# A 3x3 convolution with max-pooling: 23 of 32 steps with four products, sums from PSUM, and a new order

## The chip, the cores and the metric

The kernel runs on one core of one Trainium2 chip. The metric is the device time of one execution in microseconds (us), the median of several runs; less is better.

## The reference

16 images of 64 channels and 64x64 pixels are convolved with 128 filters of 3x3 (zero padding of one), and each 2x2 block of the result is reduced to its maximum, all in fp32:

```
x_pad = np.pad(x, ((0, 0), (0, 0), (1, 1), (1, 1)))
conv[b, co] += weight[co, ci, kh, kw] * x_pad[b, ci, kh:kh+h, kw:kw+w]     # over ci, kh, kw
output[b, c, i, j] = max of conv[b, c, 2*i:2*i+2, 2*j:2*j+2]               # 16 x 128 x 32 x 32
```

## The kernel before

**Steps.** Two images lie side by side in the 128 partitions (2 x 64 channels). A pair of images is cut into four quarters of 16 rows (eight pairs of rows, R = 8), which makes 8 x 4 = 32 steps. TensorE works on the two images (halves h = 0 and 1) at the same time, each with 64 rows of its array; a result of 128 filters x 8 rows x 64 columns fills one of eight PSUM banks (`acc`).

**Products.** A step needs the convolution's even rows and odd rows. Three taps (kw = 0, 1, 2) with one set of weights and one operand make a *product*: three matmuls for each half, six in all. Written plainly a step would have six products (two output rows by three kh); the kernel shares work between the two rows in two ways:
- a **K step** has five products. PA1 and PA2 make one difference of the outputs and PB1 and PB2 the other, straight from bf16 rows (`kx`), with weights D2, G0, D0, G2. PR adds the common part from `ks`, the sum of an even and an odd row (KS, VectorE, line 301), after the maximum of the two has been taken.
- a **W step** has four: P2 (weights GM, operand `we`, the difference of even and odd rows), P0 and P3 (weights G0 and G2, operand `wd`, differences of rows two apart) and P1 (weights GP, operand `ws`, the sum of even and odd rows). The operands are made from fp32 rows (`wx`): E makes `we` (on VectorE for the steps in `DIFF_ON_VECTOR`, else POOL, line 332), D makes `wd` (POOL, line 341), WS makes `ws` (VectorE; line 315 as a reduction over pairs for the steps in `SUM_BY_REDUCTION`, else line 323 as a sum of two SBUF operands).

**After the products.** For each half of a step: SE (W steps, line 411) is a copy of P2's bank into a second bank by ScalarE, to which P0 or P3 add. EV (lines 399 and 401) copies one bank to SBUF (`ev`) by ScalarE, with the sign changed in W steps. MX (line 427, VectorE) takes the maximum of the other bank and `ev`, in place. PR or P1 adds the common part. OD (line 431, ScalarE) copies the odd columns to SBUF, CM (line 437, VectorE) takes the maximum with the even columns into `o`, and `o` is stored.

**Order.** Nothing is scheduled by the compiler: `ORDER` is one list of step names, and each engine executes its own instructions in the order of the list. `PA1.2.1` is PA1 of step 2, half 1. A product is held until the other half has one too; then their matmuls alternate. The DMA queue of SP takes loads (`L`) and stores in the list's order as well; `LK` loads K rows as bf16 through POOL's queue; `LB` is a load held behind the last VectorE operation with two SBUF operands. POOL's operations are also held behind the last such VectorE operation (`on_vector` and `on_gpsimd`).

**The head.** Step 0 is a K step, the first W step (step 1 before) follows it. To start early both are done in halves of four rows:
- SP loads the weights (`wraw`), the first quarter in two parts (`kfirst`) and then, in the order of `first_loads = (1, 2,)`, the second K quarter (`ksecond`) and the first W step's rows in two parts (`wx`), whichever step comes first in number.
- The weights are combined (D2, D0, GM, GP on VectorE; g0, g1, g2 on ScalarE; GS on POOL; uG1, uGM, uGP on POOL), turned on TensorE (TD2, TG0, ...) and brought back to SBUF as bf16 (VD2, VG0, VGM, ...).
- XOa, XOb, XEa, XEb cast the first quarter's odd and even rows; X1 and X2 cast `ksecond` on ScalarE.
- F.k.part are the four products of step 0 (k = 0: D2, 1: G0, 2: D0, 3: G2), part 0 and 1; G.k.part those of the first W step (k = 0: P2, 1: P0, 2: P3).
- Ea and Eb (VectorE, line 353) and Da and Db (POOL, line 368) make that W step's operands by halves; SEa and SEb seed by halves.

These lines set the order of the first loads and the rule by which POOL waits:

```
first_loads = (1, 2,)
for s in first_loads:
    if s == KSTEPS[1]:
        nc.sync.dma_start(out=ksecond, in_=rows_of(0, klo2, khi2))
    else:
        wload(s, 0)
        wload(s, 1)
```

Of the kernel before, what the change touches and what calls it, by code (L numbers as in the profile page):

```python
# [11 lines left out]
def kernel(  # L12
# [103 lines left out]
    ksecond = const.tile([128, khi2 - klo2, W], FP32)  # L116
    first_loads = (1, 2,)
# [52 lines left out]
    def turn_out(m):  # L170
        free.append(turned[m])
        lo, hi, src = turned_cols(m)
        dst = wt[:, lo:hi, :].rearrange("p a b -> p (a b)")
        if m == "GM":
            nc.scalar.mul(dst, src, 0.5)
        elif m == "GP":
            nc.vector.tensor_scalar_mul(out=dst, in0=src, scalar1=0.5)
        elif m in ("G0", "G2"):
            nc.scalar.copy(out=dst, in_=src)
        else:  # L180
            nc.vector.tensor_copy(out=dst, in_=src)  # L181

# [85 lines left out]
    def first_product(k, part):  # L268
        s, q = KSTEPS[0], 0
        m0, first, where, skip = (  # L270
            (D2, 1, ta, None),
            (G0, -1, ta, 0),
            (D0, 0, tb, None),
            (G2, 2, tb, None),
        )[k]
        span = (0, R // 2) if part == 0 else (R // 2, R)
        start = k in (0, 2) and part == 0
        if start:
            take(where, s, 0)
            take(where, s, 1)  # L280
        pair_of_taps(where, s, m0, step2(kx_of(s), first), start, skip, span)
# [27 lines left out]

    def ws(s):  # L310
        row["ws", s] = ws_pool.tile([128, R, W], BF16, name="ws")
        t, f = wx_rows(s)
        if s in SUM_BY_REDUCTION:
# [14 lines left out]
    def we(s):  # L328
        row["we", s] = e_pool.tile([128, R, W], BF16, name="we")
        t, f = wx_rows(s)  # L330
        vector = s in DIFF_ON_VECTOR
        inst = (nc.vector if vector else nc.gpsimd).tensor_tensor(  # L332
# [43 lines left out]
    def lk(n, part):  # L376
# [3 lines left out]
        if n == 0:  # L380
            inst = kload(0, *chunk(2 + part))
            if part == 0:
                behind(inst, sbuf_op[0])
        elif part == 0:
# [8 lines left out]
    ev, od, ot, made = {}, {}, {}, {}  # L393
# [39 lines left out]
    def colmax(s, h):  # L433
# [5 lines left out]
        made[s] = made.get(s, 0) + 1  # L439
# [3 lines left out]
        if s == N - 1:  # L443
            store = nc.scalar if made[s] == 1 else nc.sync
            store.dma_start(out=dst[:, h : h + 1], in_=src[:, h : h + 1])
        elif made[s] == 2:
            nc.sync.dma_start(out=dst, in_=src)


    def cast_rows(lo, hi):  # L450
        on_vector(nc.vector.tensor_copy(out=kx[0][:, lo:hi:2, :], in_=kfirst[:, lo:hi:2, :]))  # L451

    def cast_more(first):
# [7 lines left out]
        "g0": lambda: nc.scalar.copy(out=slots(G0), in_=g0),  # L461
        "g1": lambda: nc.scalar.copy(out=slots(G1), in_=g1),  # L462
        "g2": lambda: nc.scalar.copy(out=slots(G2), in_=g2),
# [3 lines left out]
        "GM": lambda: on_vector(nc.vector.tensor_sub(out=slots(GM), in0=gsum, in1=g1)),  # L467
        "GP": lambda: on_vector(nc.vector.tensor_add(out=slots(GP), in0=gsum, in1=g1)),
        "XOa": lambda: cast_rows(1, kmid),
        "XOb": lambda: cast_rows(kmid, khi),  # L470
        "XEa": lambda: cast_rows(0, kmid),
        "XEb": lambda: cast_rows(kmid + 1, khi),
# [11 lines left out]
        "SE": seed, "EV": evac, "MX": rowmax, "OD": odd, "CM": colmax,  # L484
    }
# [4 lines left out]
    for m in PRODUCTS:  # L490
# [3 lines left out]
        D0 g2 g1 TD0 TG2 g0 D2 XEa LB.3 LB.4 PR.0.1 TD2 VG2 PA1.2.1 VD0 TG0 uG1 TG1 GS F.2.0 VD2 XOa LB.6  # L494
        LB.8 LB.9 GM VG0 F.3.0 XOb F.0.0 uGM F.1.0 VG1 F.0.1 TGM PA2.2.1 XEb LK.0.0 F.1.1 F.2.1 F.3.1 VGM GP
        Ea KS.0 Eb EV.0.1 G.0.0 EV.0.0 G.0.1 uGP P2.3.1 SEa.0 SEa.1 SEb.1 MX.0.1 Da Db TGP SEb.0 MX.0.0 VGP
        LK.0.1 X2 PR.0.0 G.1.0 X1 G.2.0 PB1.2.1 PB2.2.1 WS.1 G.2.1 G.1.1 L.11 P0.3.1 PA1.2.0 PA2.2.0 P3.3.1
        OD.0.0 OD.0.1 EV.1.0 KS.2 E.3 CM.0.1 EV.1.1 P1.1.1 D.3 CM.0.0 PR.2.1 PB1.2.0 P2.3.0 MX.1.0 PB2.2.0
        EV.2.1 P1.3.1 SE.3.1 EV.2.0 WS.3 MX.1.1 P1.1.0 SE.3.0 P0.3.0 MX.2.0 MX.2.1 EV.3.1 PR.2.0 EV.3.0 D.4
        MX.3.1 OD.2.0 PA1.5.1 OD.1.0 E.4 PA1.5.0 PA2.5.0 P3.3.0 OD.1.1 OD.2.1 L.12 L.14 PA2.5.1 OD.3.1  # L500
        P2.4.1 CM.1.1 CM.2.0 P2.4.0 CM.1.0 PA1.7.1 D.6 EV.5.0 CM.3.1 CM.2.1 MX.3.0 PA2.7.1 PB1.5.1 SE.4.0
        PA1.7.0 PA2.7.0 EV.5.1 SE.4.1 EV.7.0 PB2.5.1 P0.4.1 P0.4.0 P2.6.1 KS.7 E.6 P3.4.1 WS.4 WS.6 P1.3.0
        EV.4.0 PR.5.1 KS.5 WS.8 EV.7.1 P0.6.1 PB1.5.0 PB1.7.0 PB2.5.0 PB2.7.0 L.16 P1.4.1 EV.4.1 MX.5.1
        P3.4.0 OD.3.0 SE.6.1 MX.5.0 LK.1.0 LK.1.1 CM.3.0 MX.4.1 P3.6.1 OD.5.1 PB1.7.1 MX.7.0 PB2.7.1 PR.5.0
        OD.5.0 P2.6.0 EV.6.1 E.8 PR.7.0 MX.4.0 OD.4.1 OD.7.0 CM.5.1 D.8 P1.4.0 SE.6.0 OD.4.0 CM.5.0 E.9
        MX.6.1 CM.7.0 CM.4.0 P1.6.1 P2.8.0 CM.4.1 D.9 P2.8.1 SE.8.0 P0.6.0 P2.9.1 MX.7.1 P3.6.0 OD.6.1
        EV.6.0 P0.8.0 L.17 P3.8.0 SE.8.1 CM.6.1 PR.7.1 EV.8.0 OD.7.1 P0.8.1 MX.6.0 SE.9.1 E.11 MX.8.0 P1.6.0
        D.11 CM.7.1 P2.9.0 OD.6.0 EV.8.1 CM.6.0 WS.9 P3.8.1 P1.8.0 P0.9.1 PA1.10.1 SE.9.0 P2.11.0 OD.8.0
        L.19 L.20 P3.9.1 PA2.10.1 KS.10 EV.9.1 SE.11.0 P0.9.0 CM.8.0 E.14 P2.11.1 MX.9.1 P3.9.0 MX.8.1
        P0.11.0 EV.9.0 EV.10.1 MX.9.0 P1.9.1 D.14 E.12 P1.8.1 PA1.10.0 P3.11.0 PA2.10.0 SE.11.1 OD.9.1  # L510
        P1.9.0 P2.14.0 WS.11 CM.9.1 P0.11.1 P3.11.1 EV.11.0 EV.11.1 OD.8.1 OD.9.0 EV.10.0 P1.11.0 PA1.13.0
        PA1.13.1 MX.11.0 MX.11.1 PA2.13.1 D.12 L.22 L.23 PA2.13.0 P2.12.0 CM.8.1 CM.9.0 D.16 P1.11.1 EV.13.1
        P2.12.1 OD.11.0 SE.14.0 OD.11.1 PB1.10.1 WS.14 P0.14.0 CM.11.0 PB2.10.1 P3.14.0 CM.11.1 L.24 P0.12.0
        SE.12.1 P0.12.1 SE.12.0 P3.12.1 P3.12.0 EV.14.0 PB1.10.0 P2.14.1 WS.12 PB2.10.0 EV.13.0 MX.10.1
        EV.12.1 MX.14.0 E.16 EV.12.0 MX.12.1 PR.10.1 P1.14.0 MX.12.0 SE.14.1 OD.10.1 P1.12.0 PB1.13.1
# [78 lines left out]
```

## Time and profile before

| | |
|---|---|
| median of three runs | 104.88 us (104.57 to 104.96) |
| span of the profiled execution | 103.4 us |
| TensorE (PE) busy | 96.6 us, 93% |
| VectorE (DVE) busy | 91.9 us, 89% |
| ScalarE (ACT) busy | 82.1 us, 79% |
| GpSimd (POOL) busy | 75.7 us, 73% |
| read and written | 17.14 MB and 8.39 MB |

The page gives the profiled execution's span, from its first to its last instruction; what the timed runs have beyond it lies around the span. Busy time of an engine counts each stretch once, in which any of its instructions is at work. The costliest groups on VectorE are the row maximum (64 of 0.69 us), the column maximum (64 of 0.42), the sums `ws` (11 reductions of 1.23 and 10 of 0.72) and `ks` (11 of 0.43); on ScalarE EV (64 of 0.60), OD (64 of 0.38) and SE (40 of 0.58); on POOL `wd` (20 of 2.36) and `we` (16 of 1.27).

### The profile page before, as it was taken

Reading aid. Unit: us, or ns where it says so; the run is one execution under the profiler, and the core shown is the slowest. Engines: PE = TensorE matmul, PEld = TensorE weight load, DVE = VectorE, ACT = ScalarE, POOL = GpSimd, SP = SyncE. Lnnn points to the kernel's source line nnn. Section 1 sums busy time; section 2 is a strip of 40 time slices with the busy share of each in tenths; the row PEclk is TensorE's granted clock in tenths of the full one; section 3 lists DMA queues with packets and bytes.
Section 4 is the critical chain, followed back from the end, with each engine's and each line's share of the span. In section 5 each row is a group of like instructions: output and inputs, shape, how many; then the busy total and the mean of one; then the engine's idle time right before and its main releaser. Section 6 shows DMA issues by size and latency. Waiting matters only on the chain.

```text
span 103.4 us, 2542 instructions
## 1 busy us (share of the span) xinstructions
PE 96.6 (93%) x909; PEld 60.1 (58%) x909; DVE 91.9 (89%) x179; ACT 82.1 (79%) x181; POOL 75.7 (73%) x65
## 2 busy tenths in 40 slices
PE   6889899999999999999999999999999999999910
PEld 2366544555865565577777774556645777776500
DVE  1389899999999999999999999999989996979960
ACT  4545988986789997993887898987899898698820
POOL 6046969773995899998999997959997919970000
PEclk9999999999999999999999999999999999999998
DMA  2989999999899999999847997198699232006252
GB/s 63 265 297 283 389 319 337 384 405 270 219 212 307 304 302 292 341 356 225 175 131 210 252 381 263 51 203 271 173 158 257 80 136 101 0 13 223 74 202 102
DMA packets 13341, 23.33 MB, mean 226 GB/s; under 512 B 1040, under 2 KB 9488, under 8 KB 13328
## 3 DMA queue, kind: packets, MB, share of 16 engines
q1 hardware_dynamic: 12320, 20.68, 61.1%
q0 software_dynamic: 864, 2.36, 13.9%
q8 instruction: 7, 0.11, 0.4%
q10 hardware_dynamic: 144, 0.13, 0.4%
q14 instruction: 6, 0.05, 0.2%
HBM read 17.14 MB, written 8.39 MB: 247 GB/s over the span
## 4 chain that ended last, share of the span: by engine, by line
PE 83%; DMA 6%; DVE 5%; SPq 1%; issue 1%; DVEq 0%
PE acc L200 83%; DMA wx<-in_x_dram 6%; DVE acc L427 2%; DVE o L437 2%; DVE we L353 1%; SPq L114 0%; SPq L113 0%; SPq L109 0%; DVE ks L301 0%; DVEq L589 0%; DVEq L437 0%
## 5 line engine op out<-in xcount | busy, mean ns | idle before, releaser
L200 PEld LDWEIGHTS <-wt 64*128 64x128 bf16 x876 | 57.7, 94 | 34.1 <-issue 1.6
L341 POOL TENSOR_TENSOR wd<-wx 128x1024 bf16<-128x1024 f32 x20 | 47.1, 2360 | 7.6 <-PE acc L200 2.9
L200 PE MATMUL acc<-kx,wt 64*128 64x504 bf16 (+6 forms) x288 | 50.1, 356 | 0.4 <-DVE wt L181 0.4
L200 PE MATMUL acc<-wd,wt 64*128 64x504 bf16 (+3 forms) x264 | 50.1, 367 | 0.0
L427 DVE TENSOR_TENSOR acc<-acc,ev 128x512 f32<-128x512 f32 x64 | 42.0, 693 | 0.9 <-ACT ev L401 0.3
L200 PE MATMUL acc<-we,wt 64*128 64x512 bf16 (+2 forms) x132 | 31.9, 367 | 0.0
L200 PE MATMUL acc<-ws,wt 64*128 64x504 bf16 (+1 forms) x126 | 28.7, 377 | 0.1
L401 ACT ACTIVATE ev<-acc 128x512 f32<-128x512 f32 x42 | 25.1, 608 | 2.7 <-PE acc L200 2.3
L431 ACT COPY od<-acc 128x256 f32<-128x256 f32 x64 | 22.6, 379 | 5.8 <-PE acc L200 5.2
L437 DVE TENSOR_TENSOR o<-acc,od 128x256 f32<-128x256 f32 x64 | 24.5, 416 | 2.1 <-ACT od L431 1.9
L411 ACT COPY acc<-acc 128x512 f32<-128x512 f32 x40 | 23.0, 581 | 3.0 <-PE acc L200 1.7
L332 POOL TENSOR_TENSOR we<-wx 128x512 bf16<-128x512 f32 x16 | 20.2, 1271 | 3.4 <-DVE ws L323 2.4
L200 PE MATMUL acc<-ks,wt 64*128 64x504 bf16 (+1 forms) x66 | 16.5, 377 | 0.4 <-DVE acc L427 0.4
L315 DVE TENSOR_REDUCE ws<-wx 128x512 bf16<-128x1024 f32 x11 | 13.5, 1230 | 0.0
L399 ACT COPY ev<-acc 128x512 f32<-128x512 f32 x22 | 12.9, 595 | 0.6 <-PE acc L200 0.5
L323 DVE TENSOR_TENSOR ws<-wx 128x512 bf16<-128x512 f32 x10 | 7.0, 720 | 0.0
L301 DVE TENSOR_TENSOR ks<-kx 128x512 bf16<-128x512 bf16 x11 | 4.6, 429 | 0.4 <-ACT kx L458 0.4
L551 PE MATMUL acc<-const-bfloat16-1.0 128*128 128x512 bf16 x8 | 3.3, 589 | 0.8 <-PEq L575 0.8
L95 POOL DMA_DIRECT2D kx<-in_x_dram x6 | 3.5, 587 | 0.7 <-DVE kx L451 0.7
L151 POOL COPY wq<-wq 128x64 bf16<-128x64 bf16 x3 | 0.9, 314 | 3.2 <-ACT wq L462 2.5
L465 DVE TENSOR_TENSOR wq<-wraw 128x192 bf16<-128x192 f32 x1 | 0.5, 498 | 2.6 <-DMA wraw<-in_weight_dram 2.6
L368 POOL TENSOR_TENSOR wd<-wx 128x512 bf16<-128x512 f32 x2 | 2.5, 1260 | 0.4 <-DVE we L353 0.4
(30 smaller groups left out, 22.7 us busy)
## 6 DMA issues: line engine op xcount, KB each, us to landing
out_dram<-o SPq DMA_DIRECT2D x31, 256.0 KB, 4.7
wx<-in_x_dram SPq DMA_DIRECT2D x10, 512.0 KB, 7.8
wx<-in_x_dram SPq DMA_DIRECT2D x5, 544.0 KB, 8.7
wx<-in_x_dram SPq DMA_DIRECT2D x5, 480.0 KB, 7.7
kx<-in_x_dram POOLq DMA_DIRECT2D x2, 528.0 KB, 8.5
ksecond<-in_x_dram SPq DMA_DIRECT2D x1, 512.0 KB, 8.0
kx<-in_x_dram POOLq DMA_DIRECT2D x2, 256.0 KB, 6.7
kx<-in_x_dram POOLq DMA_DIRECT2D x1, 496.0 KB, 13.1
```

Source lines behind the costliest of these rows:

```text
L200: nc.tensor.matmul(acc[t][:, i0:i1, o0:o1], wt[lo : lo + CI, tap_of(m0, kw, h), :], rows(lo, i0, i1, c0, c1), start=start and kw == 1, sto ...
L301: nc.vector.tensor_tensor(out=row["ks", s], in0=t[:, f : f + 2 * R : 2, :], in1=t[:, f + 1 : f + 2 * R : 2, :], op=ADD)
L315: nc.vector.tensor_reduce(out=row["ws", s], in_=t[:, f : f + 2 * R, :].rearrange("p (r two) w -> p r w two", two=2), axis=mybir.AxisListTy ...
L323: nc.vector.tensor_tensor(out=row["ws", s], in0=t[:, f : f + 2 * R : 2, :], in1=t[:, f + 1 : f + 2 * R : 2, :], op=ADD)
L332: inst = (nc.vector if vector else nc.gpsimd).tensor_tensor(out=row["we", s], in0=t[:, f : f + 2 * R : 2, :], in1=t[:, f + 1 : f + 2 * R : ...
L341: nc.gpsimd.tensor_tensor(out=row["wd", s], in0=t[:, f + 1 : f + 1 + 2 * R, :], in1=t[:, f - 1 : f - 1 + 2 * R, :], op=SUB)
L399: nc.scalar.copy(out=ev[s, h], in_=acc[t])
L401: nc.scalar.mul(ev[s, h], acc[t], -1.0)
L411: nc.scalar.copy(out=acc[t], in_=acc[ta[s, h]])
L427: nc.vector.tensor_tensor(out=t, in0=t, in1=ev[s, h], op=MAX)
L431: nc.scalar.copy(out=od[s, h], in_=acc[tb[s, h]][:, :, 1::2])
L437: nc.vector.tensor_tensor(out=ot[s][:, h], in0=acc[t][:, :, 0::2], in1=od[s, h], op=MAX)
```

## The change

The types of the steps go from `KWKWWKWKWWKWWKWKWWKWWKWWWWKWWKWW` to `KKWWWKWKWWKWWKWWWWKWWWWWWWKWWKWW`: 9 K steps and 23 W steps for 11 and 21, with K twice at the start. The first W step is step 2, the second quarter of its pair of images.

- Seven W steps (4, 8, 9, 14, 16, 19, 23) have their odd rows copied to a free PSUM bank by ScalarE (XC). WS reads them there, and E too in the three of them that are in `DIFF_ON_VECTOR` (8, 9, 16). Reductions are left in ten W steps, sums of two SBUF operands in six.
- `DIFF_ON_VECTOR` has five steps (8, 9, 12, 16, 25) for four.
- Two K quarters of the first pair (steps 5 and 7) are loaded in fp32 by SP (LH, into `klate`) and cast by ScalarE (XK), in place of two casting loads on POOL's queue. With nine K steps there are three LK left for six.
- XEa, XOa and XEb move from VectorE to ScalarE; VGP moves to ScalarE and VGM to VectorE.
- Pools grow: `wd` 5 to 8, `we` and `ws` 5 to 7, `ev` 7 to 8, `od` and `o` 6 to 8.
- The store of a step (ST) is an entry of its own in the list; before, it followed the step's second CM at once.
- The whole list is new. F's third product (G2) now opens its bank in place of D0. Its beginning on TensorE is TD2 TG0 F.0.0 TG2 F.1.0 TD0 F.0.1 TGM F.1.1 F.3.0 G.0.0 G.0.1 TG1 F.3.1 F.2.1 F.2.0 TGP G.2.0 G.1.0 G.1.1 G.2.1 PR.0; before it was TD0 TG2 TD2 TG0 TG1 F.2.0 F.3.0 F.0.0 F.1.0 F.0.1 TGM F.1.1 F.2.1 F.3.1 G.0.0 G.0.1 TGP PR.0 G.1.0 G.2.0 G.2.1 G.1.1.

The core of the diff:

```
-    TYPES = "KWKWWKWKWWKWWKWKWWKWWKWWWWKWWKWW"
-    DIFF_ON_VECTOR = (3, 4, 6, 11,)
+    TYPES = "KKWWWKWKWWKWWKWWWWKWWWWWWWKWWKWW"
+    DIFF_ON_VECTOR = (8, 9, 12, 16, 25,)
...
-    SUM_BY_REDUCTION = (1, 3, 9, 11, 12, 14, 16, 17, 19, 20, 22,)
+    SUM_BY_REDUCTION = (2, 3, 6, 11, 12, 17, 20, 21, 27, 30,)
+    ODD_ROWS_IN_PSUM = (4, 8, 9, 14, 16, 19, 23,)
+    TURNED_BY_SCALAR = ("G0", "G2", "GP",)
+    CAST_BY_SCALAR = ("XEa", "XOa", "XEb",)
...
-        start = k in (0, 2) and part == 0
+        start = k in (0, 3) and part == 0
...
+    def odd_rows(s):
+        t, f = wx_rows(s)
+        copied[s] = free.popleft()
+        users[s] = 2 if s in DIFF_ON_VECTOR else 1
+        nc.scalar.copy(out=acc[copied[s]], in_=t[:, f + 1 : f + 2 * R : 2, :])
+
+    def with_odd_rows(s, out, op):
+        t, f = wx_rows(s)
+        nc.vector.tensor_tensor(out=out, in0=t[:, f : f + 2 * R : 2, :], in1=acc[copied[s]], op=op)
+        users[s] -= 1
+        if users[s] == 0:
+            free.append(copied[s])
...
+    def load_late(part):
+        nc.sync.dma_start(out=klate[part], in_=rows_of(0, *chunk(2 + part)))
+
+    def cast_late(part):
+        lo, hi = chunk(2 + part)
+        nc.scalar.copy(out=kx[0][:, lo:hi, :], in_=klate[part])
...
+    def store(s, h=None):
...
     ORDER = """
+        g2 g0 D2 XOa TD2 TG0 D0 GS VD2 XEa VG0 GM F.0.0 uGM LB.3 g1 TG2 XEb F.1.0 LH.0 XOb LB.6 TD0 uG1 GP LB.4
+        KS.0 F.0.1 TGM Ea VGM Eb F.1.1 VG2 uGP VD0 F.3.0 G.0.0 G.0.1 EV.0.1 TG1 EV.0.0 F.3.1 WS.2 F.2.1 F.2.0
+        LB.9 Da SEa.1 VG1 SEa.0 Db TGP SEb.1 SEb.0 LH.1 X2 MX.0.0 VGP X1 MX.0.1 G.2.0 WS.3 G.1.0 G.1.1 PR.0.0
+        E.3 G.2.1 PR.0.1 EV.2.0 EV.2.1 MX.2.0 OD.0.0 D.3 PA1.1.0 PA1.1.1 PA2.1.0 OD.0.1 PA2.1.1 XK.0 P2.3.0
...
```

More of the change, by code (lines that the diff above doesn't have):

```diff
@@ L331, in we @@
         vector = s in DIFF_ON_VECTOR
+        if vector and s in ODD_ROWS_IN_PSUM:
+            with_odd_rows(s, row["we", s], SUB)
+            return
         inst = (nc.vector if vector else nc.gpsimd).tensor_tensor(
@@ L379, in lk @@
         half = 2 * R * 2 + 1
[L380 to L384, printed above, removed]
+        if part == 0:
             kload(n, 0, min(last, half))
@@ L442, in colmax, with cast_rows @@
         src = ot[s].rearrange("p b h w -> p b (h w)")
[L443 to L446, printed above, removed]
+        if h is None:
             nc.sync.dma_start(out=dst, in_=src)
[L450 to L451 removed]
+        else:
+            (nc.scalar, nc.sync)[h].dma_start(out=dst[:, h : h + 1], in_=src[:, h : h + 1])
+    def cast_rows(n, lo, hi):
+        if n in CAST_BY_SCALAR:
+            nc.scalar.copy(out=kx[0][:, lo:hi:2, :], in_=kfirst[:, lo:hi:2, :])
+        else:
+            on_vector(nc.vector.tensor_copy(out=kx[0][:, lo:hi:2, :], in_=kfirst[:, lo:hi:2, :]))
     def cast_more(first):
@@ L466 @@
         "GS": lambda: on_gpsimd(nc.gpsimd.tensor_tensor(out=gsum, in0=g0, in1=g2, op=ADD)),
[L467 to L472, printed above, removed]
+        "GM": lambda: tap_sum("GM", GM, SUB),
+        "GP": lambda: tap_sum("GP", GP, ADD),
+        "XOa": lambda: cast_rows("XOa", 1, kmid),
+        "XOb": lambda: cast_rows("XOb", kmid, khi),
+        "XEa": lambda: cast_rows("XEa", 0, kmid),
+        "XEb": lambda: cast_rows("XEb", kmid + 1, khi),
         "X1": lambda: cast_more(0),
@@ L493 @@
     ORDER = """
[L494 to L503, printed above, removed]
@@ L547 @@
+        ST.31.1
     """
```

143 lines of the change are left out of this document (84 added, 59 removed).

## The prediction

> **What bounds the kernel now.** I read the chain that ended last first, in order of time; then the busy time by stage; then the instructions of the head and the DMA issues. Columns of the chain: start, length (us), what.
>
> ```profile
> 2.11 6.46 DMA wx<-in_x_dram
> 8.57 0.02 issue
> 8.59 0.42 DVE we L353
> ...
> 10.99 64.95 PE acc L200 x609
> 75.94 0.02 issue
> 75.96 20.42 PE acc L200 x186
> 96.38 0.03 issue
> ```
>
> Up to 8.57 the span hangs on one load, the first part of the first W step's rows; VectorE's first difference follows it by 0.02 us. From 10.99 to 96.38 nothing but the products stands in the chain.
>
> ```profile
> 20.00:30.00 10.00, 10.00 (x96) 6.51 (x94) 9.86 (x22) 7.68 (x18) 7.76 (x7) 1.00 0.97 291
> 40.00:50.00 10.00, 10.00 (x96) 6.57 (x94) 10.00 (x18) 7.63 (x18) 9.49 (x7) 1.00 0.99 288
> 80.00:90.00 10.00, 10.00 (x96) 7.16 (x94) 8.88 (x19) 8.30 (x19) 7.73 (x5) 1.00 0.24 84
> 98.00:103.40 5.40, 0.68 (x5) 0.09 (x1) 1.80 (x6) 0.99 (x4) 0.00 (x0) 0.93 0.42 146
> ```
>
> Busy time by stage (PE, weight loads, DVE, ACT, POOL, clock, DMA share, GB/s): TensorE is never free; VectorE has 0.1 us to spare until 50, 1.1 late. Busy could still hide stalls, so I counted starts: 646 of the 64-row matmuls start between 20 and 90, 0.1083 us each. A product (three taps, two halves, six matmuls) is 0.65 us, and 139 of them are 90.4 of the 92.5 us from the first product (6.22) to the last end (98.68).
>
> ```profile
> 9.81 2.49 POOL L368 TENSOR_TENSOR wd<-wx 128x512 bf16<-128x512 f32 x2 [0.37 <-DVE we L353]
> 10.99 0.82 PE L200 MATMUL acc<-ks,wt 64*128 64x512 bf16 x6 [0.43 <-DVE acc L427]
> 11.70 1.49 PE L200 MATMUL acc<-wd,wt 64*128 64x256 bf16 x24
> ```
>
> In the head, POOL's two half-differences of the first W step (Da, Db) follow VectorE's (Ea, Eb), and the step's wd products follow those. The first K step's PR product fills TensorE's wait for them.
>
> **The change, part by part.**
>
> *Products.* K steps go from 11 to 9, W from 21 to 23: 9x5 + 23x4 = 137 products. Two fewer at 0.65 are **-1.30 us**, all on the chain, since TensorE bounds from 11 to 96.
>
> *The head.* The second step is now K and the third W, so the load of ksecond (512 KB) is issued ahead of wx's two parts; before, wx's parts went first. Loads of SP's queue landed in order of issue: kfirst at 5.5 and 6.2, wx at 8.57 (320 KB) and 9.05, ksecond at 11.1. So wx's first part (again 10 rows, 320 KB) waits for 512 KB more. From below: all 832 KB behind kfirst at 405 GB/s, the page's fastest slice, land at 6.2 + 2.1 = 8.3. From above: ksecond's own 2.0 us after its forerunner give 10.6. I take 512 KB at 389 GB/s, the slice from 10.3 to 12.9: 1.3 us, so 8.57 + 1.3 = 9.9.
> From there, with rows of this page: Ea 0.42; VGM, moved from ScalarE to VectorE between Ea and Eb, 0.27 more (from start to start; a 384-element copy takes 0.34); Eb 0.45, ending at 11.0. Da and Db take 2.49, ending at 13.55. In the new order G.1.1 and G.2.1 stand ahead of PR.0 on TensorE, so PR.0 no longer fills this wait: 0.65 for the two, done at 14.2. TensorE then has finished F (4 products) and G (3). In before's trace 102 matmuls had started by 14.2: 90 of F, G and PR.0 (8 products) and 12 more, 2 products. It is behind by 3 products, 1.95 us, less 0.1 for the last still running: **+1.85 us**. Of this 1.3 is the load and 0.5 the place of PR.0. TensorE never catches up, as it is full afterwards in both.
> The rest of the head hides in that wait. Casts XOa, XEa, XEb go from VectorE (0.28 to 0.36) to ScalarE ahead of VG0 and VG2; by ScalarE's rows for 256 and 512 elements (0.38 and 0.60) they are 0.4 each and push G2's taps to about 8.0, so F.3.0 ends near 8.5, still before 9.9. F.3.1, F.2.0 and F.2.1 (under 1 us) wait for VD0, which stands behind Eb, and run while POOL makes Da and Db. Without the late load these casts would cost about 0.3.
>
> *VectorE.* KS 11 to 9: -0.86. Sums: reductions 11 to 10, -1.23; two-SBUF sums 10 to 6, -2.88; seven from PSUM. The trace has no such sum; VectorE's 0.42 (256 elements from PSUM and SBUF) and the reduction's 1.23 bound it, and the row maximum (512, one operand in each memory, 0.69) is nearest: +4.83. Differences on VectorE 4 to 5: +0.69. Casts: -1.04. Sum -0.5: 91.4 us. On its own it would allow the shorter span only because of its spare time after 70.
>
> *ScalarE.* Seeds +4 at 0.58: +2.3. Seven copies of odd rows to PSUM: between 0.38 (od) and 0.63 (the cast from SBUF), nearest the PSUM-writing seed, 0.58: +4.1. XK's casts of 1024 and 960 elements: 0.63 plus 0.22 for each 256 more: +2.1. Three casts +1.3. VGP comes and VGM goes: 0. Sum +9.8: from 82.1 to 91.9. From 14 to 94 it was busy 68.7 of 80, so 7 or 8 us more fit, with 3 to 4 left. Each copy also holds one of eight PSUM banks while its readers are due.
>
> *POOL.* Two more wd at 2.36, one more we at 1.27, three fewer DMA issues at 0.59: +4.2. From 11.05 it has 77.6 us of work (22 wd, 17 we, Da, Db, 3 issues). The last wd is due five pairs of products before TensorE's end, near 96.2, so it may idle 7.5. It idled 10.0 between 14 and 92.4 before, of which 3.3 was waiting for TensorE to release buffers; those pools grow from 5 to 8 and 7, which leaves 6.7. It fits by 0.8. Along the way, in the new order, D.4, D.12 and D.14 are due 1 to 2 us after a POOL that never idles delivers them. I put **+0.25 us** on all stalls from 14 to 96, between 0 (TensorE 79.98 busy of 80 before) and 2.5 (all 10.0 of POOL's idle time kept), nearest to the former.
>
> *Queues.* SP takes two 512 and 480 KB K loads off POOL; bytes are the same. Stores become steps of their own and many are issued late, behind loads that wait for wx rows. With eight o buffers the store of step 11, for example, must land before CM.16; I get 6 us or more between issue and reuse, against 4.7 median to landing: 0, at worst a few tenths, inside the +0.25.  The tail has the same last ten pairs of products but for their partners, and the same OD, CM, store sequence: 0, within 0.3 either way.
>
> **Sum.** 103.4 - 1.30 + 1.85 + 0.25 = 104.2 us of span. The profiled execution gives only its span; the median of the runs is 104.88, so 1.48 lies around it: **105.7 us**.
>
> **Rivals.**
> 1. *The load is hidden (not slower).* If ksecond's packets run at 405 GB/s, wx lands at 8.3; the head then loses only 0.25 and the products' saving stands: 103.4 - 1.30 + 0.25 + 1.48 = 103.8, or 104.1 with the middle's 0.25. It decides below a landing of about 9.1, where head and middle lose together what the products save. For it: of the packets of wx's first part in the trace of before, most took 0.10 us for 2560 bytes, 400 GB/s over 16 engines; six took 1.6 to 2.2 us, and only these kept the load from that rate. Against: they stalled at 4.4 to 4.8, when ksecond's packets would stand in their place and meet the same.
> 2. *POOL, or a PSUM bank, bounds the middle.* If POOL idles as long as before, wd of the steps around 14 is late and the products wait, 1 to 2.5 us; with 1.5 in place of the 0.25: 107.0. For it: the 0.8 of margin. Against: POOL waited 6.0 us for VectorE in before (2.4 + 1.7 + 1.4 + 0.5), and in this code it waits only behind VectorE's two-SBUF operations, 25 before, 17 after.
> The Trainium skill, page "SBUF — State Buffer", section "Who interferes with whom", says that a VectorE instruction with two SBUF inputs shuts out a GpSimd instruction that reads SBUF and one with a single SBUF input does not; a sum at 74.07 that ran 0.29 us beside a wd took 0.84 instead of 0.69, which agrees. By that rule POOL's 6.0 shrinks to 4.1 and this rival falls.
> 3. *The clock falls in the longer gap.* In the last row above the clock is 0.93 over 5.4 us; the trace's clock falls to 0.5, so it did for the last 0.75, 4.0 us after the last product's end at 98.68. The gap from F.3.0 (8.5) to G.0.0 (10.7) is 2.2. Should it reach 4, wx landing near 11.7, the following products run at half rate for some 3 to 4 us: 1.8 for that lateness and 1.5 to 2 for the clock, 109.
> The Trainium skill, "TensorE: Matmul & The Clock Gate", section "What's actually happening", puts the fall after at least one idle window of about 3.4 us; by that the gap is still too short.
>
> **How the numbers follow.** Forecast 0.54, load hidden 0.25, middle bound 0.18, clock 0.03. The range leaves out the clock and the far end of the middle's case: 103.8 to 107.2. A measurement of this kernel tells about 0.5% (0.52 us) from no change. Below 104.36 lies most of the hidden load: 0.25. From 104.36 to 105.40 lies the forecast's lower part, a landing of 9.2 to 9.6: 0.20. Above: 0.55.
>
> **What would show it.** Right: ksecond lands before wx's first part; Ea starts at 9.6 to 10.3, G.1.1 near 13.5; TensorE busy about 10 of 10 from 15 on, with 411 pairs instead of 417; ScalarE near 92. Wrong: Ea before 9.1 (rival 1); holes in TensorE's rows after 20 with POOL or ScalarE as releaser (rival 2); PEclk under 9 in slices 4 to 6 (rival 3).

## The result and the profile after

The changed kernel takes **107.36 us** (median of 6 runs, 106.66 to 108.21), the kernel before 104.83 us beside it (104.32 to 105.28): ratio 1.0252, 95% interval 1.0206 to 1.0299. It is slower, as forecast, but by 2.5 us instead of 0.8, and outside the range, which ended at 107.2. The profiled execution took 107.24 us with a span of 105.5. Here and below times are medians of all runs, while ratios are of means and leave out runs more than 1.5% above their kernel's fastest (one with KS.10 ahead of D.14, three with KS.10 as a reduction, one with only the loads of steps 19 and 21 moved), so that the two need not agree.

The chain of the changed kernel, in order of time (start, length, what):

```profile
2.60 6.78 DMA wx<-in_x_dram
9.38 0.02 issue
9.40 0.42 DVE we L394
...
12.63 24.84 PE acc L220 x240
...
42.12 0.68 DVE ws L340
42.80 1.30 DVE ks L321
44.10 0.62 issue
44.72 0.51 DVE ws L361
...
45.79 20.07 PE acc L220 x180
65.86 0.59 ACT ev L445
...
69.18 26.61 PE acc L220 x240
```

The head is as foreseen: the span hangs on wx's first part until 9.38. What is new stands behind it. Before, the chain was products alone from 10.99 to 96.38; now VectorE's operations stand in it from 37.5 to 45.8, a sum of 1.30 us among them, and ScalarE's copies near 66 to 69.

The first part of the page, and the busy time from 14 to 94 (window, length, PE, weight loads, DVE, ACT, POOL, clock, DMA share, GB/s), first of the changed kernel:

```profile
PE 97.8 (93%) x897; PEld 51.6 (49%) x897; DVE 93.8 (89%) x177; ACT 89.0 (84%) x197; POOL 80.2 (76%) x65
...
14.00:94.00 80.00, 78.91 (x721) 41.57 (x717) 78.30 (x144) 73.90 (x164) 71.25 (x41) 1.00 0.71 230
```

then of the kernel before:

```profile
14.00:94.00 80.00, 79.98 (x743) 50.24 (x739) 77.02 (x147) 68.69 (x153) 68.43 (x40) 1.00 0.78 229
```

TensorE stood still for 0.02 us of the 80 before and for 1.09 now; VectorE has 1.7 us left instead of 3.0, ScalarE 6.1 instead of 11.3. Busy hides the smaller stalls, so I counted starts again. The first 90 of the 64-row matmuls are F, G and PR.0; after them, 90 matmuls are 15 products.

| | before | after | difference | forecast |
|---|---|---|---|---|
| 91st matmul starts | 13.02 | 14.53 | +1.51 | +1.85 |
| two products fewer | | | -1.31 | -1.30 |
| rest of the middle: 129 products to the last one's end | 84.35 | 86.82 | +2.47 | +0.25 |
| after the last product's end | 4.71 | 4.12 | -0.59 | 0 |
| span | 103.4 | 105.5 | +2.1 | +0.8 |

(84.35 is before's 85.66 us for 131 products, for 129.) The middle is the step that failed. Per 90 matmuls it reads 9.76 9.64 9.65 9.72 9.70 9.69 10.05 9.73 before, and 9.73 9.69 **10.61 10.39 10.05 10.24** 9.88 9.64 after. Each pair of matmuls, from its start to the next pair's, less what a pair of its width takes where TensorE runs without a stop, shows where: 0.90 us at 43.5 and 0.59 at 45.0, then 0.34 at 59.3, 0.29 at 68.7, 0.11 at 70.3 and crumbs, 2.77 us in all against 0.38 before. Those two figures differ by 2.39, nearly the whole 2.47. The first two stops end with P0.14 and P2.12, the next three with products that wait for a seed.

The timeline of the changed kernel from 38 to 48, VectorE's lines (start, length, engine, line, operation, tiles; in brackets the idle time before and its releaser):

```profile
42.12 0.68 DVE L340 TENSOR_TENSOR ws<-wx,acc 128x512 bf16<-128x512 f32 x1
42.71 2.09 DVE L321 TENSOR_TENSOR ks<-kx 128x512 bf16<-128x512 bf16 x1
44.72 0.68 DVE L361 TENSOR_TENSOR ws<-wx 128x512 bf16<-128x512 f32 x1
45.32 0.74 DVE L481 TENSOR_TENSOR o<-acc,od 128x256 f32<-128x256 f32 x2
```

and POOL's in the same stretch, with two of TensorE's:

```profile
39.85 4.66 POOL L382 TENSOR_TENSOR wd<-wx 128x1024 bf16<-128x1024 f32 x2
45.48 4.68 POOL L382 TENSOR_TENSOR wd<-wx 128x1024 bf16<-128x1024 f32 x2 [0.97 <-DVE ws L361]
...
44.56 0.37 PE L220 MATMUL acc<-wd,wt 64*128 64x512 bf16 x1 [0.58 <-POOL wd L382]
45.79 0.37 PE L220 MATMUL acc<-we,wt 64*128 64x512 bf16 x1 [0.40 <-DVE o L481]
```

(A bracket gives less than the stop from start to start, as the ends of matmuls are modelled.)

KS.10, a sum of two SBUF operands that takes 0.42 elsewhere, took 2.09. It began 0.54 us into D.14, the second wd of POOL's pair (42.17 to 44.51), and ended just after it. No wait is shown for it: the time is *inside* the instruction. WS.14 ahead of it, with its second operand in PSUM, ran beside POOL at 0.68. Nothing in the program keeps the two apart: `on_gpsimd` holds a POOL operation behind VectorE's last such sum ahead of it in the list, but nothing holds VectorE behind POOL, and D.14 stands ahead of KS.10.

The late D.14 reaches TensorE in two ways. P0.14, which needs D.14's rows, started at 44.56, 0.05 after D.14's end: the stop of 0.90. And everything behind KS.10 on VectorE came 1.6 us late: WS.15, for which POOL's D.16 waits, and the column maxima that set banks free, for which P2.12 waited until 45.79: the stop of 0.59. VectorE alone would have held P2.12 until 45.79, so each way hides behind the other, and to cure one need not save much.

Why was D.14 so late? POOL had stood 0.86 us behind KS.1 at 18, and 1.61 us for a load before E.17:

```profile
31.58 2.95 POOL L373 TENSOR_TENSOR we<-wx 128x512 bf16<-128x512 f32 x2 [1.61 <-DMA wx<-in_x_dram]
```

The second of these two differences, E.15, took 1.65 instead of 1.27, as VectorE's E.12, with two SBUF operands as well, had begun 0.28 us before it. From there to D.14's end POOL never stood.

The theory to test, then: **VectorE's sums of two SBUF operands are shut out while a POOL difference is at work, and POOL is late because a load is.** The rivals: it is ScalarE or the PSUM banks, which the copies of odd rows load; or the late head alone, which shifts everything behind it; or POOL's lateness holds TensorE directly, and the sums matter little.

### The profile page after: what moved, and what is told of

It is laid out like the page before. It is cut to its first block, busy times and chain, and to the rows that moved or that the text cites. A ratio compares the mean times of both kernels' runs of the same rounds, so it can differ in the third digit from the quotient of the medians.

```text
span 105.5 us, 2533 instructions
## 1 busy us (share of the span) xinstructions
PE 97.8 (93%) x897; PEld 51.6 (49%) x897; DVE 93.8 (89%) x177; ACT 89.0 (84%) x197; POOL 80.2 (76%) x65
## 4 chain that ended last, share of the span: by engine, by line
PE 71%; DVE 11%; DMA 6%; ACT 3%; issue 3%; SPq 2%; DVEq 0%
PE acc L220 70%; DMA wx<-in_x_dram 6%; DVE acc L471 4%; DVE o L481 2%; DVE ks L321 1%; ACT acc L455 1%; ACT ev L445 1%; DVE ws L353 1%; DVE ws L361 1%; DVE ws L340 1%; ACT od L475 1%; PE acc L171 1%; ACT ev L443 0%; SPq L127 0%; DVE we L394 0%
## 5 line engine op out<-in xcount | busy, mean ns | idle before, releaser
L220 PEld LDWEIGHTS <-wt 64*128 64x128 bf16 x864 | 48.8, 94 | 44.8 <-issue 5.4
L220 PE MATMUL acc<-wd,wt 64*128 64x504 bf16 (+3 forms) x288 | 56.9, 368 | 0.7 <-POOL wd L382 0.6
L382 POOL TENSOR_TENSOR wd<-wx 128x1024 bf16<-128x1024 f32 x22 | 51.7, 2362 | 2.8 <-DVE ws L361 2.0
L220 PE MATMUL acc<-kx,wt 64*128 64x504 bf16 (+6 forms) x240 | 42.6, 356 | 0.3 <-ACT kx L496 0.3
L220 PE MATMUL acc<-we,wt 64*128 64x512 bf16 (+3 forms) x144 | 32.3, 368 | 1.5 <-DVE wt L187 1.1
L220 PE MATMUL acc<-ws,wt 64*128 64x512 bf16 (+1 forms) x138 | 32.7, 376 | 0.2 <-DVE acc L471 0.2
L220 PE MATMUL acc<-ks,wt 64*128 64x504 bf16 (+1 forms) x54 | 13.4, 377 | 0.0
L340 DVE TENSOR_TENSOR ws<-wx,acc 128x512 bf16<-128x512 f32 x7 | 4.8, 679 | 0.0
L336 ACT COPY acc<-wx 128x512 f32<-128x512 f32 x7 | 4.1, 599 | 0.1
L171 PE MATMUL acc<-ident,wq 128*128 128x128 bf16 x25 | 3.0, 257 | 0.0
```

Of the source, the lines that this page charges most:

```text
L220: nc.tensor.matmul(acc[t][:, i0:i1, o0:o1], wt[lo : lo + CI, tap_of(m0, kw, h), :], rows(lo, i0, i1, c0, c1), start=start and kw == 1, sto ...
L340: nc.vector.tensor_tensor(out=out, in0=t[:, f : f + 2 * R : 2, :], in1=acc[copied[s]], op=op)
L382: nc.gpsimd.tensor_tensor(out=row["wd", s], in0=t[:, f + 1 : f + 1 + 2 * R, :], in1=t[:, f - 1 : f - 1 + 2 * R, :], op=SUB)
```

## The experiments

Ratios are to the kernel before on the same chip, with 95% intervals; the traces are of one execution each.

**The head undone.** wx ahead of the fp32 K quarter, as before.

```
-    first_loads = (1, 2,)
+    first_loads = (2, 1,)
```

> The changed kernel, with the first W step's rows loaded ahead of ksecond, as before the change. Theory A (the late load is what the head loses): wx's first part lands near 8.6 in place of 9.4 and Ea, G.0.0 and PR.0 move up by as much; the time falls by 0.7 to 0.9 us, to 106.5 (ratio to before 1.016). Rival (the order of the head's instructions, not the load, sets when PR.0 comes): Ea moves up, but PR.0 and the end stay within 0.3 us, 107.1 or more.

106.52 us, 1.0172 (1.0134 to 1.021): 0.8 us sooner, as theory A expected, though the interval just touches the changed kernel's. The trace is of a longer run (107.12). In it Ea started at 7.45 and the 91st matmul at 13.06, 1.47 sooner, but POOL stood 2.7 us for the same load, until 31.65, KS.10 took 2.20, and the third stretch was 11.71. The 361st matmul started at 44.46 against 44.56: in that execution the middle took back nearly all that the head had won. The loss in the middle is there without the late head, so the head alone is not its cause.

**KS.10 ahead of D.14.** D.14 is then held behind it.

```
-        D.14 ... MX.11.0 P1.11.1 SE.14.0 WS.14 KS.10 OD.11.1
+        ... MX.11.0 KS.10 D.14 P1.11.1 SE.14.0 WS.14 OD.11.1
```

> The changed kernel with two entries of the list moved: VectorE's KS.10 goes ahead of WS.14, and POOL's D.14 stands behind KS.10 in the list, so that POOL waits for it. Theory B (KS.10, with two SBUF operands, was shut out by D.14 for 1.65 us, and the products behind it waited): KS.10 takes 0.42 in place of 2.09, D.14 starts 0.3 to 0.5 later, TensorE's loss between 40 and 50 shrinks by 1 us or more, and the time falls by 0.9 to 1.5 us, to 106.2 (ratio 1.013). Rival C (POOL is simply late with the operands of step 14 and after): D.14 comes later still, and the time stays or grows by up to 0.4 us, 107.4 to 107.8.

107.66 us, 1.0249 (1.0207 to 1.0291): nothing won, as rival C expected. VectorE's lines, POOL's and TensorE's say why:

```profile
41.98 0.42 DVE L321 TENSOR_TENSOR ks<-kx 128x512 bf16<-128x512 bf16 x1
...
42.91 2.47 DVE L361 TENSOR_TENSOR ws<-wx 128x512 bf16<-128x512 f32 x1
...
42.48 2.35 POOL L382 TENSOR_TENSOR wd<-wx 128x1024 bf16<-128x1024 f32 x1 [0.39 <-DVE ks L321]
...
44.89 0.37 PE L220 MATMUL acc<-wd,wt 64*128 64x512 bf16 x1 [1.03 <-POOL wd L382]
```

KS.10 takes its 0.42, and the next such sum, WS.15, is shut out in its place. D.14, held 0.39 us behind KS.10, comes later still, and P0.14 with it: TensorE's two stops are 1.36 and 0.24 instead of 0.90 and 0.59.

**KS.10 with one operand**, as a reduction over pairs of rows.

```
+        if s in KS_BY_REDUCTION:                      # (10,)
+            nc.vector.tensor_reduce(out=row["ks", s], in_=t[:, f : f + 2 * R, :]
+                .rearrange("p (r two) w -> p r w two", two=2), axis=X, op=ADD)
+            return
```

> The changed kernel with KS.10 alone as a reduction over pairs of rows, one SBUF operand in place of two; order and all else stay. Theory B: the reduction runs its own 1.23 us beside D.14, so KS.10 is 0.85 us shorter than the 2.09 it took; the time falls by 0.5 to 0.9 us, to 106.7 (ratio 1.018). Rival C, or a KS.10 that is long for another reason such as its data: no gain, 107.3 or more, and KS.10 takes over 1.5 us still.

107.24 us, 1.0161 (1.0112 to 1.021), runs from 105.71 to 108.65: unclear in time, but the trace (of the fastest run) tells the two ways apart:

```profile
41.62 1.21 DVE L323 TENSOR_REDUCE ks<-kx 128x512 bf16<-128x1024 bf16 x1
...
38.69 4.66 POOL L392 TENSOR_TENSOR wd<-wx 128x1024 bf16<-128x1024 f32 x2
...
43.40 0.37 PE L221 MATMUL acc<-wd,wt 64*128 64x512 bf16 x1 [0.58 <-POOL wd L392]
```

Beside D.14 (41.00 to 43.35) the reduction took 1.21, its own time; WS.15, which met the last of D.14, took 1.15. P0.14 still waited for D.14, 0.83 us, while the stop at P2.12 fell from 0.59 to 0.24. Third and fourth stretch 20.5 instead of 21.0. So a KS.10 that is not shut out is worth some 0.4 us here; most of the rest is D.14 being late for TensorE.

**No sums from PSUM.** All seven copies taken out; the sums and the three differences on VectorE read two SBUF operands.

```
-    ODD_ROWS_IN_PSUM = (4, 8, 9, 14, 16, 19, 23,)
+    ODD_ROWS_IN_PSUM = ()                             # and no XC in the list
```

> The changed kernel without the odd rows in PSUM: no XC, the seven sums and three differences read two SBUF operands. ScalarE loses 4.1 us of work and a PSUM bank is free more often. Theory B: ten more VectorE operations with two SBUF operands meet POOL's and are shut out for 0.5 to 1.5 us each; the time rises by 3 to 8 us, to 110 to 115. Rival D (ScalarE, at 89 of 105 us, and the PSUM banks bound the middle): the time falls by 0.5 to 1.5 us, to 106 to 107.

114.68 us, 1.0949 (1.092 to 1.0978). ScalarE is 3.2 us freer and no bank is held for odd rows, yet 7.3 us are lost, within theory B's 3 to 8: whatever the copies cost ScalarE and the banks is less than what they save VectorE. Thirteen sums of two SBUF operands averaged 1.06 us instead of 0.73; one of them met both wd of a pair:

```profile
45.91 3.07 DVE L361 TENSOR_TENSOR ws<-wx 128x512 bf16<-128x512 f32 x1
...
43.78 4.66 POOL L382 TENSOR_TENSOR wd<-wx 128x1024 bf16<-128x1024 f32 x2
```

**Four ways to have POOL on time.** First E.17 behind D.15; then this with wx first; then both with the head's list as before (VD0 ahead of Ea, F ahead of G, PR.0 ahead of G.2); and, by itself, the load of step 17 ahead of those of 15 and 16.

```
-        PR.7.1 E.17 P2.8.1          ...  EV.12.0 D.15 P2.16.0
+        PR.7.1 P2.8.1               ...  EV.12.0 D.15 E.17 P2.16.0
```

> The changed kernel with one entry of the list moved: POOL's E.17, due only near 55, from between D.8 and E.15 to behind D.15. Theory P (POOL stands at E.17 until its far-ahead load lands at 31.6, and this sets when D.11, D.12 and D.14 come): E.15 starts near 30, D.14 ends near 43 in place of 44.5, KS.10 is locked out for 0.3 in place of 1.65, the third stretch of 90 matmuls falls from 10.6 to 9.7 to 10.0, and the time falls by 1.0 to 1.8 us, to 106 (ratio 1.011). Rival B' (wherever POOL stands, some two-operand sum of VectorE falls on a wd of 2.36 us): D.14 is earlier, but another of VectorE's sums is locked out and the time stays within 0.4 us.

> E.17 moved as in the first, and the first W step's rows loaded ahead of ksecond. Theory P: without the stop at E.17 the head's gain is no longer given back at 35 to 45; the two add up, the 91st matmul starts near 13.1 and the third stretch is at most 10.0: 105.2 to 105.6 (ratio 1.004 to 1.008). Rival: the head's gain is given back elsewhere: no better than either alone by more than 0.3 us, 106 or more.

> As the second, and the head's list as before the change: VD0 and VGM ahead of Ea, all of F ahead of G, and PR.0 ahead of G.2 to fill TensorE's wait for Da and Db. Theory (half a microsecond of the head is the place of PR.0): the 91st matmul starts 0.4 to 0.7 earlier than in the second kernel and the time falls by as much, to 104.8 (ratio 1.000). Rival (after the head POOL and the loads set the pace): the 91st matmul is earlier, but the time stays within 0.3 us of the second kernel's.

> The changed kernel with the load for step 17 issued ahead of those for 15 and 16; POOL's order stays, E.17 included. Theory P: E.17 finds its rows at 30 and starts 1 to 1.6 us earlier, E.15 may wait for its own a little, D.14 comes about 1 us earlier and the time falls by 0.5 to 1.2 us, to 106.5 (ratio 1.016). Rival (it is the time that E.17 takes on POOL, 1.27 us, not its wait): no gain, 107.2 or more.

107.72 (1.0287, 1.0246 to 1.0327), 107.20 (1.0223, 1.019 to 1.0256), 107.43 (1.0248, 1.021 to 1.0285) and 107.12 (1.0236, 1.0195 to 1.0277), where 104.8 to 106.5 were expected: none helps. In the third the head's list did not pay either. The 91st matmul came 0.14 us sooner than in the second instead of 0.4 to 0.7: VG1 stands ahead of Eb in that list and waited 0.67 us for TensorE, so Da started 1.86 after Ea instead of 1.15. In all four POOL stood as long, 1.7 to 2.9 us until about 32. With E.17 out of the way it was E.15 that waited, for a row that step 14's load brings (landed 31.84). The sums that met a wd changed: KS.10 2.02 and KS.13 1.57 in the first, KS.13 1.29 in the third with KS.10 at 0.70. Not one load or entry is late, but all of them between 24 and 34. So I read when the loads were issued and landed in the changed kernel, in its order of issue; the last column is of a later experiment:

| load (MB) | issued | landed | landed, loads in order of use |
|---|---|---|---|
| step 12 (0.54) | 12.02 | 21.43 | 20.94 |
| step 19 (0.51) | 16.60 | **22.71** | 37.07 |
| step 11 (0.48) | 16.97 | 24.48 | 22.14 |
| step 15 (0.51) | 17.95 | 26.40 | 24.02 |
| step 16 (0.48) | 18.45 | 29.21 | 25.24 |
| step 17 (0.54) | 18.93 | 31.51 | 27.55 |
| step 14 (0.51) | 20.11 | 32.72 | 28.78 |
| K pair, casting (1 read) | 22.20 | 31.71 | 33.87 |

From 12 to 22 SP's loads, the fp32 K rows among them, land 1.2 to 1.3 us apart without a gap: SP's queue is full, and the DMA share is 1.02 to 1.06 from 14 to 34 (0.90 to 1.06 before). Step 19's load, first read at 51.9 us by XC.19 (not at 56, as the next expectation has it), stands ahead of five that are due sooner; beside the K pair's casting load the others come 2 to 3 us apart.

**The loads in the order of use.** Steps 19 and 21 loaded behind step 22; the same with wx first; and the first with the K pair's load one wd later, too.

```
-        WS.6 L.19 PB2.1.1 ...  P2.4.0 L.21 MX.5.0  ...  L.22 P3.9.1
+        WS.6 PB2.1.1      ...  P2.4.0 MX.5.0       ...  L.22 L.19 L.21 P3.9.1
-        KS.5 LK.1.0 OD.3.0 ...  D.6 EV.4.1                # the third only
+        KS.5 OD.3.0        ...  D.6 LK.1.0 EV.4.1
```

> The changed kernel with the wx loads of steps 19 and 21 (each 0.5 MB, used at 56 us and later) issued behind that of step 22 instead of ahead of those of steps 11, 15, 16 and 17. In the changed kernel the loads land one behind the other without a gap from 12 to 34 us, the one of step 19 at 22.71, ahead of those of steps 11 (24.48), 15 (26.40), 16 (29.21) and 17 (31.51), and GpSimd stands 1.61 us for that of step 17. Theory Q (the transfers set when GpSimd gets its operands, GpSimd runs late by what it stood, and its late D.14 then shuts out the sum KS.10): loads 11, 15 and 16 land 1.2 us sooner and that of 17 at about 30.3; GpSimd stands 0.4 us or less before 32; D.14 begins at about 40.9 instead of 42.2 and the sum at 42.7 takes under 1.0 us instead of 2.09; third and fourth stretch of 90 matmuls together 20.1 or less instead of 21.0; time 106.5, ratio 1.016. Theory S (how far GpSimd stands makes no difference, the sums lose to whichever wd is beside them): GpSimd stands less but the same time is lost at the next sums, 107.2 to 107.5. Theory T (the transfers are not the limit, the casting load of the next K pair alone is): load 17 still lands after 31, GpSimd stands over 1.2 us, 107.3.

> As the kernel before this one, and the first wx load ahead of the fp32 K quarter again, as the kernel before has it. Theory Q: the head's 0.7 to 1.3 us is now kept, since GpSimd no longer stands for a load: 91st matmul at 13.0 to 13.9, third and fourth stretch together 20.1 or less, time 105.8, ratio 1.009. Theory S: 106.6 to 107.2 as with the wx load first alone (ratio 1.017).

> As the first of these, and the casting load of the K pair of steps 10 and 13 (1 MB read, issued at 22.2 and landed at 31.7, while the loads that land beside it are 2.8 us apart instead of 1.3) issued one wd later, at about 25.5. Theory Q: load 17 lands at 29 or before, GpSimd stands not at all before 32, D.14 begins at 40.5 or before, third and fourth stretch 20.0 or less, 106.3, unless the K pair comes late: then the products of step 10 wait at 36 to 38 and the third stretch is 10.3 or more. Theory S: 107.2 to 107.5.

107.32 (1.0219, 1.0149 to 1.029), 106.00 (1.015, 1.0095 to 1.0206), **106.24** (1.0153, 1.0117 to 1.0188, four runs within 0.5 us). The first alone is unclear in time. In its trace, of its longest run (108.00), step 17 landed at 28.09, but step 14 only at 32.32, beside the K pair, and POOL stood 1.23 us for it; D.14 came 0.5 us sooner, KS.10 took 0.69 and third and fourth stretch were 20.1, as theory Q has it, but the second, fifth and sixth were 0.4 to 0.7 longer. The second came near its expected 105.8. The third came as expected, and its interval lies below the changed kernel's (1.0206 to 1.0299). In it all land in time (the table's last column). Its POOL waits from 13 to 46 (engine, line, releaser, us, times, longest) no longer hold a load:

```profile
POOL wd L382 <- DVE ws L361: 1.0, 1, 1.0
POOL we L373 <- DVE ks L321: 0.8, 1, 0.8
POOL wd L382 <- DVE ks L321: 0.7, 1, 0.7
POOL we L373 <- DVE we L373: 0.3, 1, 0.3
```

and its VectorE and POOL pass each other:

```profile
42.60 0.67 DVE L321 TENSOR_TENSOR ks<-kx 128x512 bf16<-128x512 bf16 x1
43.19 0.68 DVE L361 TENSOR_TENSOR ws<-wx 128x512 bf16<-128x512 f32 x1
...
38.31 4.68 POOL L382 TENSOR_TENSOR wd<-wx 128x1024 bf16<-128x1024 f32 x2
```

The pair of wd ends at 42.99 instead of 44.51, KS.10 meets its last 0.4 us and takes 0.67. Third and fourth stretch: 20.1 instead of 21.0 (20.0 expected). The two stops of 0.90 and 0.59 are gone together. The time, however, fell by 1.0% only: 0.34 at 58.1 and 0.29 at 67.5 stayed, and 0.49 at 46.0 and 0.25 at 34.8 came, both at products that wait for a seed.

**Two copies fewer for ScalarE**, and head and middle together. In that third kernel TensorE's 0.49 at 46 ends with a seed, and ScalarE runs without a gap from 40 to 47, with copies of odd rows at 41.1 and 44.4. Steps 14 and 19 become reductions; then wx first without this; then both.

```
-    ODD_ROWS_IN_PSUM = (4, 8, 9, 14, 16, 19, 23,)
+    ODD_ROWS_IN_PSUM = (4, 8, 9, 16, 23,)              # 14 and 19 to SUM_BY_REDUCTION
```

> The kernel with the later loads (steps 19 and 21, and the K pair), and in it the sums of steps 14 and 19 as reductions, so that ScalarE has two copies of 0.6 us fewer (at 41.1 and near 52) and VectorE two operations of 1.23 us for two of 0.68. Theory A (ScalarE runs back to back there, 40 to 47 without a gap, and the seed that TensorE awaits at 46 is late by the copies in front of it): the gap of 0.49 us at 46 falls to 0.1 or less, that of 0.34 at 58 to 0.2 or less, those at 67 to 69 stay; fourth stretch of 90 matmuls 9.8 instead of 10.26; 105.6, ratio 1.010. Theory V (VectorE, as full as ScalarE, only hands the wait on): the gaps stay or grow, 106.2 to 106.9.

> The kernel with the later loads, and the first wx load ahead of the fp32 K quarter. If head and middle add up: 91st matmul at 13.0 to 13.8 instead of 14.1, the other stretches as they were, 105.5, ratio 1.009. If the gain of the head is lost to the next wait: 106.2 again.

> Both edits together. If they add up: 105.0, ratio 1.004; by theory V 105.5 to 106.5.

106.77 (1.0206, 1.0138 to 1.0274), **105.91** (1.011, 1.0065 to 1.0155), 106.80 (1.0189, 1.0128 to 1.0251). The gap at 46 did go. The seed, SE.12, ended 0.42 us sooner without the copy, but TensorE also came 0.2 later to it, as a gap of 0.39 had opened at 43.9; so the copies are part of its cause, and the trace does not show that they are all of it. VectorE, with 1.23 for 0.68 twice, now stands in the chain where it had not, 46.5 to 51.2 with hardly a break, and gaps of 0.44 and 0.37 opened at 52.1 and 56.0. The expectation of 105.6 was wrong; the wait was handed on, as theory V says. Both edits together missed even theory V's 105.5 to 106.5. wx first was worth 0.3 us in the medians (0.4 by the ratios) of an expected 0.7: in its trace the 91st matmul was 1.19 sooner (12.95 against 14.14), yet the last product ended 0.11 sooner. Of that, 0.49 went at 18, where E.4 had waited 1.3 us for its load and then shut out KS.1:

```profile
16.55 1.13 DVE L321 TENSOR_TENSOR ks<-kx 128x512 bf16<-128x512 bf16 x1
...
16.13 1.27 POOL L373 TENSOR_TENSOR we<-wx 128x512 bf16<-128x512 f32 x1 [1.28 <-DMA wx<-in_x_dram]
```

No kernel tried beats the one before.

## Why the prediction was wrong, step by step

- **Products, -1.30: right.** 864 matmuls for 876, and undisturbed stretches run at the same 9.64 to 9.73.
- **Head, +1.85: right in mechanism, 0.34 too large.** The load was given 1.3 and cost 0.8 (Ea 9.40 for 8.59); 9.38 lies 1.1 above the bound from below. From Ea to the 91st matmul it is 5.12 to 5.21 in all nine traces with this order of loads, against 4.43 before: the rest is 0.7, where 0.5 was put down to the place of PR.0. That fits, since PR.0's 0.65 now stands behind Db, but the one experiment with PR.0 in its old place moved Db too and does not show it. "TensorE never catches up" is not a rule: the median of the first experiment kept the head's 0.8, but the middle has stalls of its own, and in two traces with wx first most of what the head had won was lost there (the first experiment's, and 1.08 of 1.19 us with the loads moved).
- **Middle, +0.25: the step that failed; it was 2.47.** It rests on a POOL that delivers in time. POOL's work was forecast right (80.2 us busy, 79.9 by the prediction's sum), but not where its stops fall. The prediction gave D.14 1 to 2 us of room over a POOL that never idles, and POOL had stood 2.5 us by then, 1.6 of them for a load. So D.14 was late, and 1.49 us went at P0.14 and P2.12: the first waited for D.14 itself, the second for VectorE, whose KS.10 D.14 had shut out. That these come from the late D.14 is shown: with the loads moved both stops are gone. About 0.7 more are three stops at seeds, which no experiment took apart, and the rest is crumbs.
- **Rival 2, the bound middle (0.18), is what came,** nearly in its own words: "wd of the steps around 14 is late and the products wait, 1 to 2.5 us". Two arguments spoke against it, and both failed. POOL's waits for VectorE behind the head were to shrink from 6.0 to 4.1, as 17 operations hold it for 25; they came to 6.0 again (2.0, 1.6, 0.9, 0.8 and 0.7 by releaser). And I had used half a rule. The Trainium skill, page "SBUF — State Buffer", section "Who interferes with whom", says that a VectorE instruction with two SBUF inputs contends with a POOL instruction that reads SBUF, and that issue order decides who blocks. I used it only for VectorE blocking POOL. The runs agree with both directions: 0.42 became 2.09 beside a wd that had begun first, E.15 took 1.65 for 1.27 behind E.12, and sums with one SBUF operand kept their time beside a wd (0.68, 1.21). The row that the prediction quotes as agreeing already showed the direction that it left out: the sum at 74.07 took 0.84 beside a wd that had begun at 72.01. Fewer such operations are no relief if the few meet POOL.
- **Queues, "bytes are the same ... 0": wrong.** Not the bytes but their order and time mattered: behind the first W step's two, the new list has 13 wx loads issued by 29 us where the old one had 9, with two for after 50 us among them (steps 19 and 21). This is what made POOL late; putting order and the K pair's time right together was worth 1.0%, the order alone is unclear in time.
- **ScalarE "7 or 8 us more fit": wrong as it was argued.** It has room over 80 us (73.9 busy) and, in the kernel with the loads moved, none from 40 to 47. Busy came to 89.0 for 91.9; neighbours on ScalarE overlap by 0.1 (a seed of 0.57 and the next start 0.48 later). The durations of the new operations were right (groups: busy, mean ns; the first line is of the kernel before, the others of the changed one):

```profile
L301 DVE TENSOR_TENSOR ks<-kx 128x512 bf16<-128x512 bf16 x11 | 4.6, 429 | 0.4 <-ACT kx L458 0.4
...
L321 DVE TENSOR_TENSOR ks<-kx 128x512 bf16<-128x512 bf16 x9 | 5.8, 656 | 0.2 <-ACT kx L496 0.2
L340 DVE TENSOR_TENSOR ws<-wx,acc 128x512 bf16<-128x512 f32 x7 | 4.8, 679 | 0.0
L361 DVE TENSOR_TENSOR ws<-wx 128x512 bf16<-128x512 f32 x6 | 4.4, 730 | 0.0
L336 ACT COPY acc<-wx 128x512 f32<-128x512 f32 x7 | 4.1, 599 | 0.1
```

  0.69 and 0.58 were taken for the sum from PSUM and the copy. Only `ks` is off its 0.43, by nine times 0.23 us, of which KS.10 alone is 1.67. That is most of why VectorE was busy for 93.8 us instead of 91.4.
- **Tail, 0: 0.59 sooner.** Before, five column maxima in a row (1.74 us) followed the last wait; now one of 0.42 does.
- **Rivals 1 and 3.** In the changed kernel's trace Ea started at 9.40, past the 9.1 below which the load was to count as hidden. But in seven of the nine traces with this order it started before 9.1 (mean 8.93), and the load still cost 0.9 and not 0.25, measured against 8.06 with wx first; so the sign was badly placed, and one trace could not decide it. The clock did not fall in the changed kernel's head.

What stays open: the gaps near 59 and 69 (0.6 us together) were not taken apart. They stood in every trace of the new list, also without the sums from PSUM (0.24 and 0.29 there), so they do not hang on the copies of odd rows. Both end with a seed. In the changed kernel SE.17 started at 59.20, as the last matmul of P2.17 ended (59.19), with one product between P2.17 and P0.17 in the list; SE.21 stood behind an EV while P2.21 had ended 0.78 us earlier. That points at the order of the list, but no run tests it. And whether wx first is worth its 0.3 us is not settled: the intervals of the two kernels overlap.

## What to carry to other kernels

Where two engines shut each other out, as VectorE's sums of two SBUF operands and POOL's differences do here, price each such instruction by what the other engine has running when it starts, in both directions, and look for the loss in an instruction's own length as well as among the waits. Where an operand has 1 to 2 us of room, add up the stops of its engine ahead of it, loads included, before calling the room enough. Issue loads in the order of use once the queue is full, since one load for later delays every load behind it. When engines have little of their time left, expect a cured wait to reappear on the next one, and do not add up gains from the head and the middle.

## What the runs showed of the hardware

- A sum of two SBUF operands that meets a POOL difference already at work lasts beyond its end: 2.09, 2.47 and 3.07 us for 0.42 and 0.68. KS.10 (bf16) ended 0.29 after D.14, the two fp32 sums 0.54 and 0.56 after the wd, so they did most of their work behind it. The one of 3.07 had met the last 0.2 us of D.12 and did not get in ahead of D.14, which followed at once. Reductions (1.21 to 1.26) and sums or differences with a PSUM operand (0.67 to 0.71) were not touched in any of the sixteen traces.
- The same load lands at other times from one execution to the next: Ea started between 8.35 and 9.43 in nine traces with the changed order of loads (mean 8.93), and between 7.45 and 8.57 in six with wx first (mean 8.06). So the load's price is 0.9 on average, and one trace alone can be off by half a microsecond.
- The clock is a term of the head that a single trace does not show. The record of full clock begins at 3.56 to 6.68 us in fifteen of sixteen traces (3.71 before, 6.68 after), and matmuls of 256 columns ahead of it take 0.41 us for 0.27. In the last kernel's trace it begins at 9.51: the 91st matmul started at 14.59, which is 6.7 and not 5.1 after Ea. In the second kernel with the loads moved the clock fell within the head, as the row from 8 to 10 shows:

```profile
8.00:10.00 2.00, 2.00 (x19) 1.00 (x19) 1.10 (x4) 0.67 (x2) 0.35 (x2) 0.50 1.09 315
```

  TensorE had stood 1.63 us for a cast, and the 91st matmul came 1.7 us later than Ea and the usual 5.13 would put it. The stretches of full clock are whole multiples of 3.413 us in all the traces (1, and 27 to 31). The Trainium skill, page "TensorE: Matmul & The Clock Gate", section "What's actually happening", gives such a free-running window of 3413 ns; the traces agree, but here the fall followed a window (4.51 to 7.92) in which TensorE had worked 1.77 of 3.41 us, not an idle one.
